# Two quarters of W_out laid out directly behind the second piece of y, in the first frame pair of the output projection

## The chip, the core and the metric

The kernel runs on one core of one Trainium2 chip. The time is the device time of one execution in microseconds (us), taken from the runs listed below; the profile is one further execution, recorded instruction by instruction. Engines are named as in the profile: PE is TensorE (PEld its weight loads), DVE is VectorE, ACT is ScalarE, POOL is GpSimd, SP is SyncE, which here only issues DMAs.

## The reference, cut to what matters

One layer of a streaming trunk is computed for 2048 prompt frames and 32 sample frames, all in float32:

```
proj = rmsnorm(h, g_mix) @ w_in              # 1024 -> 3072, split into hA bA cA zA vB zB
y    = concat[conv_mixer(hA, bA, cA, zA), pool_mixer(vB, zB)]      # 1024 wide
h    = h + y @ w_out                         # 1024 x 1024   <- the stage of this change
gate = sigmoid(rmsnorm(h, g_ple) @ w_ple_gate)
h    = h + (p @ w_ple) * gate
out  = rmsnorm(h, g_final)
```

The outputs are the normalised frames and the last rows of the two mixers' histories.

## The kernel before, in words

**Products.** Every float32 operand of a large product is split in two reduced-precision parts, hi and lo: ACT casts hi (`split`, L78), DVE subtracts it from the source for lo (L79). A product is then three matmuls: hi·hi, hi·lo, lo·hi. The 1024x1024 weight is cut into quarters 11, 12, 21 and 22, and two frame tiles of 128 frames are taken together, so that Strassen's scheme (Winograd's form) needs seven half products in place of eight. `frame_parts` (L181) makes the seven frame operands of a pair, called pieces here: the plain 11, 12, 22 and the sums S1 to S4. `weight_sums` makes the weight sums T1 to T4; the plain quarters 11, 21 and 22 of the weight are laid out without a sum.

**Order within a pair.** `seven` (L211) issues the products of one pair into three PSUM banks X, Y, Z, 12 matmuls each. With its argument late set and for the first pair (in_parts set) the order is:

1. X = piece 11 with W11 (L163); ACT copies X out (L1199), called here the first copy-out
2. the call of step 1, then half of Z = S1 with T1
3. X += S2 with T2; ACT copies X out again (L1199), the second copy-out
4. the rest of Z; third copy-out
5. X += S3 with T3, which may only begin when the second copy-out has read X; DVE adds X to the result (L1194)
6. Y = piece 12 with W21 (L163, named y_o in the profile): first the four hi·hi matmuls, then four lo·hi, then four that use the lo of W21; DVE adds Y to the result
7. Z += S4 with W22 (L163, z_o), in the same order of parts
8. X += piece 22 with T4 (L168, x_o<-wo_T), which may only begin when the add of item 5 has read X

Later pairs have the same products, all through L168.

**What the change touches.** `layout` casts and subtracts quarters of the weight: for each of four k, one ACT cast of 128x512 (L1266) and one DVE subtraction (L1267) for each quarter named. W11 is laid out first. The call of step 1 for the first pair is `rest`: it calls `more` (L204), which makes pieces 12, S4 and 22, and then lays out quarters 21 and 22, alternating between the two, eight casts and eight subtractions in all. In the profile the hi of W21 is in the tile wo_c, the lo of W21 and both parts of W22 in tiles named wo_d, the pieces are y (11, 12, 22) and y_S (S1 to S4).

**Who sets the order.** Each engine runs its own list of instructions in the order in which the program has them. That order comes from a planner, at build time: it goes through modelled time and gives an engine, when it comes free, the ready instruction that stands first in the kernel text. `tc.issue_after(ins)` pins every instruction that the block makes on the engine of `ins` behind `ins` on that engine; it holds nothing on other engines. In `rest` the ACT casts of the layout are pinned behind the cast of piece 22.

**Buffers.** The ring cmb has eight buffers of 4 KB a partition. Four hold the raw lower rows of W_out (wo_q, loaded at L323), the other four the pieces 11, S2, S1, S3, so piece 12 takes the buffer of 11 when the first product is through, S4 that of S2, and 22 that of S1. The pool w3, whose three tiles of 8 KB hold the lo of W21 and both parts of W22, is opened where the ring wr of the first stage lay (seven buffers of 4 KB); the tile for the lo of W22 lies on buffers of that ring from which the second and third output tile of the early embedding (eout) are still being stored to memory (L149). The upper and lower half of a pair's raw y are loaded by SP (L315) into a ring of five; the lower half of the first pair is read last when piece 22 is made, and its buffer then takes half of the third pair.

Of the kernel before, what the change touches and what calls it, by code (L numbers as in the profile page):

```python
# [12 lines left out]
ALU = mybir.AluOpType  # L13
# [22 lines left out]
def trunk(ctx, tc, x_p, x_s, c_conv, c_pool, p_p, p_s, g_mix, w_in, conv_w, conv_b, pool_w,  # L36
          pool_scale, w_out, g_ple, w_gate, w_ple, g_fin, y_p, y_s, sc_p, sp_p, sc_s, sp_s):
    nc = tc.nc
# [38 lines left out]
    def split(hi, lo, src, eng=nc.vector):  # L77
        ins = nc.scalar.copy(hi, src)  # L78
        eng.tensor_tensor(lo, src, hi.bitcast(F32), op=ALU.subtract)  # L79
        return ins  # L80
# [100 lines left out]
    def frame_parts(cmb, tmp, name, a11, a12, a21, a22):  # L181

        A = {}

        def put(q, src):
            A[q] = cmb.tile([P, KH, 2, P], F32R, tag="c", name=f"{name}_{q}")
            return split(A[q][:, :, 0], A[q][:, :, 1], src)  # L190

        def comb(q, x, y, op):
            t = tmp.tile([P, KH, P], F32, tag="s", name=f"{name}_f{q}")
            nc.vector.tensor_tensor(t, x, y, op=op)
            return t

        s1 = comb("S1", a21, a22, ALU.add)
        put("11", a11)
        s2 = comb("S2", s1, a11, ALU.subtract)
        put("S2", s2)  # L200
        put("S1", s1)
        put("S3", comb("S3", a11, a21, ALU.subtract))

        def more():  # L204
            put("12", a12)
            put("S4", comb("S4", a12, s2, ALU.subtract))
            return put("22", a22)

        return A, more

# [120 lines left out]
    with ExitStack() as s1:  # L331
# [17 lines left out]
        def put(piece, src):  # L349

            return split(piece[:, :, 0], piece[:, :, 1], src)
# [823 lines left out]
    with ExitStack() as s2:  # L1175
# [4 lines left out]
        def quarters(name, W):  # L1180
            c = halves(slot(f"{name}_c"))
            d = {h: w3.tile([P, KH, NH], F32R, tag=f"d{h}", name=f"{name}_d{h}") for h in (1, 0, 2)}
            W.update({"11": c[:2], "21": (c[2], d[0]), "22": (d[1], d[2])})
# [38 lines left out]
        def prep_h(i):  # L1222
            lo, hi = load_y(i, 2 * P) if i else first_y
            S[i], more = frame_parts(cmb, ss, f"y{i}", lo[:, :, :P], hi[:, :, :P], lo[:, :, P:], hi[:, :, P:])
            return more
# [35 lines left out]
        def layout(parts):  # L1261
            for k in range(KH):
                for q, t, c in ("11", tops[k // 2], k % 2), ("21", bots[k], 0), ("22", bots[k], 1):
                    if q in parts:
                        hi, src = W[q][0][:, k], t[:, c * NH:c * NH + NH]
                        nc.scalar.copy(hi, src)  # L1266
                        hold.append(nc.vector.tensor_tensor(W[q][1][:, k], src, hi.bitcast(F32), op=ALU.subtract))  # L1267

        quarters("wo", W)
        layout(["11"])  # L1270

        def rest():

            with tc.issue_after(more().ins):
                layout(["21", "22"])

        S = {}
        more = prep_h(0)
# [9 lines left out]
        for i in range(0, NT - 1, 2):  # L1288
# [5 lines left out]
            last = i + 4 == NT - 1  # L1294
# [3 lines left out]
            if i + 2 < NT - 1:  # L1298

                with tc.issue_after(loaded[-1].ins), tc.issue_after(hold[-1].ins):  # L1300
                    more = prep_h(i + 2)
# [367 lines left out]
```

## Time and profile before

| | us |
|---|---|
| three runs | 922.24, 920.8, 922.03 |
| median | 922.03 |
| the profiled execution, device time | 923.96 |
| its span, first to last instruction | 922.2 |
| PE busy in it | 907.6 |
| DVE, ACT, POOL busy in it | 723.1, 477.8, 149.9 |

The profiled execution is one run of its own: 1.76 us of its time lie outside the span. A row of the timeline gives the start, the length, the engine, the line of the kernel, the output and inputs and the number of instructions merged in it; in square brackets stands how long the engine had been idle before and what ended that. A row of the waits gives who waited for whom: the total in us, how often, the longest. Lengths of neighbouring instructions overlap by the pipeline's fill, so the distance between two starts is what an instruction costs in a row of its kind.

### The profile page before, as it was taken

The numbers are of one execution on the slowest core, as the hardware profiler recorded it, in microseconds if no ns is written. First come the engines' busy times: TensorE is split into PE (matmuls) and PEld (weight loads), VectorE is DVE, ScalarE is ACT, GpSimd is POOL, SyncE is SP. The second block draws the span as 40 slices with busy tenths as digits, with TensorE's granted clock in tenths as the row PEclk, the third lists the DMA queues.
The fourth block names the chain that finished last, engine by engine and source line by source line (L and its number), as shares of the span: only waits on it lengthen the run. The fifth ranks groups of instructions, "written<-read, shape, count | busy, mean of one in ns | idle before, by whom it ended". The sixth has DMA issues, their size and how long they took to land.

```text
span 922.2 us, 12940 instructions
## 1 busy us (share of the span) xinstructions
PE 907.6 (98%) x4485; PEld 820.7 (89%) x4485; DVE 723.1 (78%) x1231; ACT 477.8 (52%) x883; POOL 149.9 (16%) x271
## 2 busy tenths in 40 slices
PE   7999999999999999999999999999999999999996
PEld 5999999999999999999999987888877868888885
DVE  6896999999488989785777679665554799888975
ACT  6744565555335555443545456334334776465555
POOL 3111322212001111000000010111111002233333
PEclk9999999999999999999999999999999999999999
DMA  8345585769945546457655359755675876799883
GB/s 245 94 150 155 151 264 165 210 197 306 421 119 167 185 156 190 109 178 272 202 172 172 124 192 292 255 194 175 246 229 159 299 259 156 182 235 239 200 259 108
DMA packets 140734, 186.37 MB, mean 202 GB/s; under 512 B 12060, under 2 KB 111260, under 8 KB 139389
## 3 DMA queue, kind: packets, MB, share of 16 engines
q1 hardware_dynamic: 120237, 126.33, 44.7%
q0 software_dynamic: 17696, 53.71, 19.9%
q10 hardware_dynamic: 2736, 5.51, 1.8%
q8 instruction: 35, 0.57, 0.3%
q14 instruction: 30, 0.25, 0.1%
HBM read 128.93 MB, written 56.56 MB: 201 GB/s over the span
## 4 chain that ended last, share of the span: by engine, by line
PE 96%; ACT 1%; DVE 1%; DMA 1%; issue 0%; POOL 0%; SPq 0%; ACTq 0%; DVEq 0%; POOLq 0%
PE x_g L168 9%; PE x_o L168 9%; PE x_zbv L564 7%; PE x_ch L564 7%; PE x_zab L564 7%; PE e L103 5%; PE z_g L168 5%; PE z_o L168 4%; PE z_zbv L564 3%; PE z_ch L564 3%; PE z_zab L564 3%; PE v L564 3%; PE c L564 3%; PE b L564 3%; PE za L564 3%; PE h L564 3%
## 5 line engine op out<-in xcount | busy, mean ns | idle before, releaser
L78 ACT CAST y_S<-y_fS 128x512 fp32r<-128x512 f32 x32 | 19.5, 621 | 41.3 <-PE x_o L168 17.4
L103 PE MATMUL e<-wq,pps 128*128 128x512 f32 (+1 forms) x156 | 38.9, 399 | 0.2 <-ACT pps L78 0.2
L168 PE MATMUL x_o<-wo_b,y_S 128*128 128x512 f32 x128 | 35.7, 391 | 0.0
L168 PE MATMUL x_g<-wg_b,g_S 128*128 128x512 f32 x128 | 35.7, 389 | 0.0
L564 PE MATMUL z_zbv<-B,w_zbv_S 128*128 128x416 f32 x168 | 34.2, 352 | 0.0
L564 PE MATMUL x_ch<-B,w_ch_S 128*128 128x416 f32 x168 | 34.1, 351 | 0.0
L564 PE MATMUL z_zab<-B,w_zab_S 128*128 128x416 f32 x168 | 34.1, 351 | 0.0
L564 PE MATMUL x_zab<-B,w_zab_S 128*128 128x416 f32 x168 | 34.0, 351 | 0.0
L564 PE MATMUL x_zbv<-B,w_zbv_S 128*128 128x416 f32 x168 | 34.0, 351 | 0.0
L564 PE MATMUL z_ch<-B,w_ch_S 128*128 128x416 f32 x168 | 34.0, 350 | 0.0
L103 PEld LDWEIGHTS e<-wq,pps 128*128 128x128 f32 (+1 forms) x156 | 27.4, 182 | 6.9 <-ACT pps L78 0.5
L1396 POOL DMA_DIRECT2D e<-h_d x28 | 24.8, 907 | 51.1 <-DVE e L1393 42.3
L564 PEld LDWEIGHTS x_zab<-B,w_zab_S 128*128 128x128 f32 x168 | 31.3, 188 | 0.4
L564 PEld LDWEIGHTS x_zbv<-B,w_zbv_S 128*128 128x128 f32 x168 | 31.4, 188 | 0.3
L564 PEld LDWEIGHTS z_ch<-B,w_ch_S 128*128 128x128 f32 x168 | 31.4, 188 | 0.3
L564 PEld LDWEIGHTS z_zab<-B,w_zab_S 128*128 128x128 f32 x168 | 31.3, 188 | 0.3
L564 PEld LDWEIGHTS x_ch<-B,w_ch_S 128*128 128x128 f32 x168 | 31.3, 188 | 0.3
L564 PEld LDWEIGHTS z_zbv<-B,w_zbv_S 128*128 128x128 f32 x168 | 31.3, 188 | 0.4
L70 POOL TENSOR_SCALAR ms_x<-ssq_x 128x1 f32<-128x1 f32 (+2 forms) x18 | 10.7, 593 | 125.1 <-ACT junk L89 125.0
L78 ACT CAST y<-y 128x512 fp32r<-128x512 f32 x24 | 14.9, 619 | 29.3 <-PE z_o L168 12.8
L78 ACT CAST g_S<-g_fS 128x512 fp32r<-128x512 f32 x32 | 19.0, 618 | 18.6 <-DVE g_fS L1572 12.8
L168 PEld LDWEIGHTS x_o<-wo_b,y_S 128*128 128x128 f32 x128 | 24.0, 188 | 5.1 <-ACT c_o L1199 0.3
(592 smaller groups left out, 2656.6 us busy)
## 6 DMA issues: line engine op xcount, KB each, us to landing
y<-y_d SPq DMA_DIRECT2D x16, 512.0 KB, 5.6
x<-in_x_prompt_dram SPq DMA_DIRECT2D x16, 512.0 KB, 5.3
h_d<-x SPq DMA_DIRECT2D x16, 512.0 KB, 2.6
hn<-h_d SPq DMA_DIRECT2D x61, 128.0 KB, 6.5
xt<-in_x_prompt_dram SPq DMA_DIRECT2D x15, 512.0 KB, 6.1
e<-e_d SPq DMA_DIRECT2D x15, 512.0 KB, 6.0
e<-h_d POOLq DMA_DIRECT2D x28, 256.0 KB, 6.4
out_dram<-e POOLq DMA_DIRECT2D x13, 512.0 KB, 4.0
```

What stands on the lines that cost most here:

```text
L70: nc.gpsimd.tensor_scalar(ms[:n], ssq[:n], scalar1=1.0 / D, scalar2=EPS, op0=ALU.mult, op1=ALU.add)
L78: ins = nc.scalar.copy(hi, src)
L103: nc.tensor.matmul(ps[:n], pps[:, a, k, :n], wp[k][b][:, cs], start=k + q == 0, stop=k == 1 and q == 2)
L168: nc.tensor.matmul(ps[:n], lhs[:, k, a, :n], w[b][:, k], start=start and k + q == 0, stop=k == KH - 1 and q == 2, skip_group_check=True)
L564: nc.tensor.matmul(ps[:, :NB], lhs[:, k, x], b[:, k, y], start=start and k + q == 0, stop=stop and k == KH - 1 and q == 2, skip_group_chec ...
L1396: nc.gpsimd.dma_start(ee, h_d[r:r + P, at[1] * NH:at[1] * NH + NH], accum_op=ALU.add)
```

## The change

`more` takes a function that it calls between piece 12 and the pieces S4 and 22. For the first pair that is the layout of the quarters 21 and 22. Its ACT casts are pinned behind the cast of piece 12 and no longer behind that of piece 22; the ACT casts of S4 and 22 are pinned behind the last cast of the layout (`layout` now returns it). For the later pairs `more` is called without a function: there S4 and 22 are pinned behind 12.

```
-        def more():
-            put("12", a12)
-            put("S4", comb("S4", a12, s2, ALU.subtract))
-            return put("22", a22)
+        def more(then=None):
+            ins = put("12", a12)
+            if then:
+                with tc.issue_after(ins.ins):
+                    ins = then()
+            with tc.issue_after(ins.ins):
+                put("S4", comb("S4", a12, s2, ALU.subtract))
+                put("22", a22)
...
-                        nc.scalar.copy(hi, src)
+                        last = nc.scalar.copy(hi, src)
                         hold.append(nc.vector.tensor_tensor(W[q][1][:, k], src, hi.bitcast(F32), op=ALU.subtract))
+            return last
...
-            with tc.issue_after(more().ins):
-                layout(["21", "22"])
+            more(lambda: layout(["21", "22"]))
```

No instruction, byte or buffer is added or taken away.

## The prediction

> **What bounds the kernel now.** I read the page first.
>
> ```profile
> span 922.2 us, 12940 instructions
> ...
> PE 907.6 (98%) x4485; PEld 820.7 (89%) x4485; DVE 723.1 (78%) x1231; ACT 477.8 (52%) x883; POOL 149.9 (16%) x271
> ...
> PE 96%; ACT 1%; DVE 1%; DMA 1%; issue 0%; POOL 0%; SPq 0%; ACTq 0%; DVEq 0%; POOLq 0%
> ```
>
> PE is busy 98% of the span and is 96% of the chain that ended last. So a change of order, which adds no work, can only move PE's waits. The waits of PE in the whole span, and all waits between 546 and 570 us, where the first pair of W_out runs:
>
> ```profile
> PE pt L416 <- DVE xt L407: 2.9, 2, 2.3
> ...
> PE y_o L163 <- ACT wo_c L1266: 0.5, 1, 0.5
> ```
>
> ```profile
> PEld y_o L163 <- ACT wo_c L1266: 1.3, 2, 0.9
> ...
> PEld x_o L168 <- ACT c_o L1199: 0.3, 1, 0.3
> ```
>
> In this stage PE waits for two things: the layout's casts (item 6 of the order) and, a little, a copy-out. The row of 0.5 understates it, because the weight loads wait too. The true price comes from comparing stretches (columns: length, then busy time and count by engine, clock, DMA):
>
> ```profile
> 546.87:567.33 20.46, 19.91 (x86) 15.67 (x85) 17.50 (x29) 11.53 (x21) 1.98 (x3) 1.00 1.05 323
> 567.33:586.39 19.06, 19.06 (x86) 15.76 (x84) 16.49 (x27) 9.34 (x18) 3.13 (x6) 1.00 0.79 257
> ...
> 555.14:558.00 2.86, 2.86 (x13) 2.36 (x13) 2.78 (x6) 2.64 (x6) 0.00 (x0) 1.00 1.19 211
> 558.00:561.88 3.88, 3.33 (x14) 2.17 (x12) 3.88 (x7) 3.10 (x7) 0.00 (x0) 1.00 1.11 228
> 561.88:564.61 2.73, 2.73 (x14) 2.25 (x12) 2.72 (x6) 0.14 (x1) 0.00 (x0) 1.00 1.03 353
> ```
>
> The first pair takes 20.46 us, the second 19.06, at the same clock of 1.00: 1.40 us is all there is to win. A product of 12 matmuls takes 19.06 / 7 = 2.72. The stretch of y_o (558.00 to 561.88) takes 3.88: 1.16 too long. The one before it is 0.14 too long; 0.10 is spread over the rest.
>
> Why y_o is late is in the timeline, ACT first, then PE:
>
> ```profile
> 549.86 0.59 ACT L1199 COPY c_o<-x_o 128x512 f32<-128x512 f32 x1 [1.53 <-PE x_o L163]
> 550.35 0.62 ACT L78 CAST y<-y 128x512 fp32r<-128x512 f32 x1
> 553.99 0.62 ACT L78 CAST y_S<-y_fS 128x512 fp32r<-128x512 f32 x1 [3.02 <-PE x_o L168]
> 554.51 0.58 ACT L1199 COPY c_o<-x_o 128x512 f32<-128x512 f32 x1
> 555.36 0.62 ACT L78 CAST y<-y 128x512 fp32r<-128x512 f32 x1 [0.27 <-PE z_o L168]
> 555.88 0.62 ACT L1266 CAST wo_c<-wo_q 128x512 fp32r<-128x512 f32 x1
> 556.40 0.62 ACT L1266 CAST wo_d<-wo_q 128x512 fp32r<-128x512 f32 x1
> ...
> 559.53 0.62 ACT L1266 CAST wo_d<-wo_q 128x512 fp32r<-128x512 f32 x1
> ```
>
> ```profile
> 553.74 1.52 PE L168 MATMUL z_o<-wo_a,y_S 128*128 128x512 f32 x6
> 555.14 3.02 PE L168 MATMUL x_o<-wo_b,y_S 128*128 128x512 f32 x12
> 558.00 1.14 PE L163 MATMUL y_o<-wo_c,y 128*128 128x512 f32 x3
> 559.67 1.45 PE L163 MATMUL y_o<-wo_c,y 128*128 128x512 f32 x5 [0.54 <-ACT wo_c L1266]
> ...
> 564.61 2.88 PE L168 MATMUL x_o<-wo_T,y 128*128 128x512 f32 x12
> ```
>
> Piece 12 is cast at 550.35. Then ACT stands idle 3.02 us, because the next in its list, S4, wants the buffer of S2. S4 is cast at 553.99, the second copy-out runs at 554.51, piece 22 waits for S1's buffer until 555.36, and only behind it come the eight casts, 0.52 apart (555.88 to 556.40). The hi of W21 for the last k is the seventh, from 555.88 + 6 x 0.52 = 559.0 on; PE wants it at about 558.00 + 3 x 0.23 = 558.7.
>
> **The change part by part.** *The eight casts* (L1266, no DMA among them) move into the idle time. Their start is 550.35 + 0.52 = 550.87 and their end 550.87 + 8 x 0.52 = 555.03, so every hi of W21 and W22 is there before y_o at 558. Their raw rows must have landed:
>
> ```profile
> 541.00 1.97 SPq L323 DMA_DIRECT2D wo_q<-in_w_out_dram  x4
> ```
>
> ```profile
> DMA to landing us min/median/max: 3.6/4.6/5.5
> ```
>
> The last issue ends at 542.97; with the longest landing 548.5, over 2 us early. Term: -1.16, if all of y_o's excess goes; bounds 0 and -1.40.
>
> *What is late next on ACT.* The casts are longer than the hole: it ended at 553.99, they end at 555.03. The second copy-out stands last in the text, and S4 is ready with it, so I expect S4 at 555.03 and the copy-out at 555.55: 1.04 later than its 554.51. If piece 22 also gets ahead (its buffer frees at 555.26, when z_o ends), 1.56 later; if the copy-out comes straight behind the casts, 0.52; if it gets between them, nothing. The x_o at 555.14 has no slack: the 0.3 above is its wait for this copy-out. So as PE's list stands now the price is +0 to +1.56. But PE's list is planned too, and y_o, with all its hi casts done, is ready in that gap. That the planner fills so is in the trace of an earlier stage, where the transpose pst stands ahead of product b in the text, was late, and came after eight of its matmuls:
>
> ```profile
> 533.49 1.76 PE L564 MATMUL b<-hn,w_b 128*128 128x416 f32 x8
> 535.08 0.27 PE L988 MATMUL pst<-ident,st 128*34 128x128 f32 x1
> 535.11 3.27 PE L564 MATMUL b<-hn,w_b 128*128 128x416 f32 x16
> ```
>
> I take +0.16 for a cut product and imperfect filling, near the lower end because of these rows; both ends stay in the range.
>
> *S4 and 22 behind the casts.* Piece S4 is cast about 1 us later, 22 about 0.7 to 1.2. They are wanted by z_o (before: 561.88) and by x_o<-wo_T (564.61): over 4 us of cover, cost 0. The third copy-out comes earlier.
>
> *DVE.* The eight subtractions follow the casts. One of them meets a new wait: the lo of W22 goes where an embedding tile is still being stored.
>
> ```profile
> 548.32 0.55 POOL L149 DMA_DIRECT2D e_d<-eout  x1 [10.34 <-ACT y_S L78]
> ```
>
> ```profile
> e_d<-eout POOLq DMA_DIRECT2D x1, 512.0 KB, 7.1
> ```
>
> ```profile
> 557.22 0.69 DVE L1267 TENSOR_TENSOR wo_d<-wo_q,wo_d 128x512 fp32r<-128x512 f32 x1
> ...
> 560.84 0.68 DVE L1267 TENSOR_TENSOR wo_d<-wo_q,wo_d 128x512 fp32r<-128x512 f32 x1
> 561.44 0.68 DVE L1194 TENSOR_TENSOR x<-x,c_o 128x512 f32<-128x512 f32 x1
> ...
> 562.69 0.68 DVE L1194 TENSOR_TENSOR x<-x_o,x 128x512 f32<-128x512 f32 x1
> ```
>
> Before, that subtraction ran at 557.22, past the landing at 548.32 + 7.1 = 555.4. Now its cast is done by 552, and DVE stands at it until 555.4. Queued behind: seven subtractions counting itself, then S4's and 22's, two adds of copies, the add of Y, and the add of X. At 0.60 apiece (557.22 to 560.84 is six steps) the add of X starts at 555.4 + 12 x 0.60 = 562.6, as before (562.69). The lo of W21 is complete at 555.4 + 6 x 0.60 = 559.0, 559.1 with the pipeline; PE wants its last part at 558.00 + 11 x 0.23 = 560.5. The add of X must end, at 563.3, before x_o<-wo_T may start, which starts at 564.61 now: at best 1.3 earlier. So DVE costs nothing at a gain of 1.16, but it caps the gain.
>
> *SP.* No DMA moves in the text. But the load of the lower half for the third pair waits for piece 22's subtraction, which followed the cast of 555.36 and now comes at about 560.3; it waits at the head of SP's queue:
>
> ```profile
> 555.65 1.48 SPq L315 DMA_DIRECT2D y<-y_d  x2
> 565.90 0.33 SPq L1220 DMA_DIRECT2D h_d<-x  x1
> ```
>
> ```profile
> y<-y_d SPq DMA_DIRECT2D x2, 512.0 KB, 11.7
> ```
>
> ```profile
> 570.86 0.68 DVE L194 TENSOR_TENSOR y_fS<-y,y 128x512 f32<-128x512 f32 x1
> ```
>
> It goes out at about 561 instead of 556.8. Its first reader runs at 570.86. At the landing time of 11.7 it would come at 572.7, 1.8 too late; I take nothing, since 11.7 is the half queued behind two loads of x, and half the bytes of that backlog are gone by 561. SP's next issue is due at 565.90, past that. POOL gets and loses nothing. Later pairs already cast in the order 12, S4, 22, so their pins cost 0.
>
> **Sum.** -1.16 + 0.16 = -1.0. The profiled execution's 923.96 would be 922.96. Its time is 1.93 above the median of the runs, 922.03, so for the median I say 921.0.
>
> **The rivals.** *The copy-out binds* (0.22). PE keeps its list, x_o waits for the copy-out behind eight casts and one or two pieces: +1.04 to +1.56 against -1.16 to -1.30, hence -0.26 to +0.40, a median of 921.8 to 922.4. For it: the copy-out had no slack before. Against it: the filling rows. [...]
>
> *DVE held by the store* (0.10, the slower side). The place is the first subtraction of W22's lo; the price is one us for each us that the store lands after 555.4, as the whole list behind it, with the add of X at its end, shifts. From a landing at 556.7 on, nothing is left of the gain. At the 11.7 us that the y loads take it would land at 560.0: +4.6 - 1.2 = +3.4, or 925.4. For it: DMA share stands over 1.0 in these stretches. Against: the store is issued before anything that moves, so 7.1 should hold.
>
> *The late half for the third pair* (0.06): DVE is held at 570.86 for up to 1.8, of which PE feels at most 1.3: net about +0.3, 922.3.
>
> *The change does not do what it says* (0.05): the casts come no earlier, 922.0. Only missing raw rows could do it.
>
> **How the numbers follow.** Forecast 0.57: 921.0, by its own bounds (-1.40 to -0.5) 920.6 to 921.5. Runs of before lie 1.4 apart, so a median may be off by some 0.6. The range 919.9 to 923.0 leaves out the far part of the DVE rival and unlucky draws. A measurement of this kernel tells some 0.2%, 1.84 us, from no change; the whole excess of the pair is 1.40, so faster by more needs a further gain or luck: 0.11. Slower by more is the DVE rival past 558.5, or a knock-on of the new plan: 0.08. Within: 0.81.
>
> **What would show it.** Right: casts of L1266 from about 550.9 to 555.0 behind the cast of y; no wait of y_o on wo_c; the stretch of the first pair at 19.2 to 19.9 us. The copy-out rival shows as x_o (L168) waiting for ACT c_o by about 1 us with y_o behind it. The DVE rival shows as an idle time ahead of a wo_d subtraction ended by e_d's DMA and a late x_o<-wo_T. What would make me wrong: a PE wait outside this pair that before did not have, from a different plan downstream.

## The result, and the profile after

| | before | after |
|---|---|---|
| median of 8 runs each, us | 922.13 (920.8 to 923.77) | 926.09 (924.79 to 928.84) |
| ratio to before, 95% interval | | 1.0045 (1.003 to 1.006) |
| profiled execution, its span | 923.96, 922.2 | 925.96, 924.2 |

The change makes the kernel slower by about 4.0 us, outside the range of the prediction. The head of the page after shows no more work; PE is busy for 906.0 us where it was 907.6:

```profile
span 924.2 us, 12940 instructions
...
PE 906.0 (98%) x4485; PEld 818.9 (89%) x4485; DVE 722.8 (78%) x1231; ACT 477.1 (52%) x883; POOL 151.5 (16%) x271
```

The waits of PE between 540 and 595 us name what is new. The wait of y_o for the weight's casts is gone, and three others stand in its place:

```profile
PE x_o L168 <- DVE c_o L1198: 1.9, 1, 1.9
PE x_o L168 <- ACT c_o L1203: 1.0, 1, 1.0
PE x_o L168 <- DVE x L1198: 0.7, 1, 0.7
```

The same stretches as before, by the starts of the pairs, and then the second pair in pieces. The columns are the window, its length, busy time and count of PE, PEld, DVE, ACT and POOL, then the granted clock, the DMA share and GB/s:

```profile
544.72:566.10 21.38, 19.70 (x86) 15.67 (x85) 17.03 (x28) 11.63 (x22) 1.98 (x3) 1.00 1.01 305
566.10:588.98 22.88, 20.96 (x86) 16.83 (x84) 17.08 (x28) 10.74 (x20) 3.89 (x7) 0.93 0.68 223
...
570.20:572.26 2.06, 0.14 (x2) 0.00 (x1) 2.06 (x5) 2.06 (x5) 1.21 (x2) 1.00 0.93 267
572.26:574.00 1.74, 1.74 (x5) 1.39 (x6) 1.74 (x3) 0.88 (x2) 0.02 (x1) 0.69 0.96 272
574.00:575.30 1.30, 1.30 (x4) 0.99 (x3) 0.01 (x1) 0.00 (x0) 0.00 (x0) 0.50 1.04 340
```

The first pair takes 21.38 us (20.46 before), the second 22.88 (19.06): together +4.74. The larger part lies in the second pair. There the change only pins the casts of S4 and 22 behind that of 12, and ACT has these casts in the same order before and after. The spans differ by only 2.0, mainly because the first pair of the profiled execution of before began 2.15 later, at 546.87; the other 0.6 lies behind the two pairs. In the fourteen profiles of this study the first pair begins between 544.72 and 547.29. The sum of the two pairs is free of that, and is the measure used below; each is read from one profiled execution.

**First pair.** ACT, then DVE, then PE of the kernel after:

```profile
548.72 0.61 ACT L1270 CAST wo_c<-wo_q 128x512 fp32r<-128x512 f32 x1
...
552.36 0.62 ACT L1270 CAST wo_d<-wo_q 128x512 fp32r<-128x512 f32 x1
554.02 0.62 ACT L78 CAST y_S<-y_fS 128x512 fp32r<-128x512 f32 x1 [1.04 <-DVE wo_d L1271]
554.55 0.61 ACT L78 CAST y<-y 128x512 fp32r<-128x512 f32 x1
555.07 0.58 ACT L1203 COPY c_o<-x_o 128x512 f32<-128x512 f32 x1
```

```profile
553.29 0.69 DVE L1271 TENSOR_TENSOR wo_d<-wo_q,wo_d 128x512 fp32r<-128x512 f32 x1 [2.88 <-DMA e_d<-eout]
...
561.29 0.69 DVE L194 TENSOR_TENSOR y_fS<-y,y 128x512 f32<-128x512 f32 x1 [1.28 <-DMA y<-y_d]
561.90 0.69 DVE L79 TENSOR_TENSOR y<-y,y 128x512 fp32r<-128x512 f32 x1
562.51 0.68 DVE L1198 TENSOR_TENSOR x<-x_o,x 128x512 f32<-128x512 f32 x1
...
571.52 0.69 DVE L1198 TENSOR_TENSOR c_o<-x_o,x 128x512 f32<-128x512 f32 x1
```

```profile
552.95 1.75 PE L163 MATMUL y_o<-wo_c,y 128*128 128x512 f32 x7
555.70 3.01 PE L168 MATMUL x_o<-wo_b,y_S 128*128 128x512 f32 x12 [1.00 <-ACT c_o L1203]
...
563.25 3.02 PE L168 MATMUL x_o<-wo_T,y 128*128 128x512 f32 x12 [0.68 <-DVE x L1198]
...
572.26 0.50 PE L168 MATMUL x_o<-wo_a,y_S 128*128 128x512 f32 x1 [1.92 <-DVE c_o L1198]
```

The casts run in the old hole of ACT, from 4.00 us after the pair's start on. But the second copy-out comes behind S4 and 22, 10.35 us after the start (555.07 - 544.72; before 554.51 - 546.87 = 7.64). S4 stands ahead of it for 1.04 us, ended by a subtraction of the layout on DVE. From this release I infer that in the program after, S4 has the buffer of a raw row of the weight, wo_q, and no longer that of S2: that row is read last by the subtraction at 553.29, which stood 2.88 us for the embedding's store. The planner did fill PE: seven matmuls of y_o go ahead. They end at 552.95 + 7 x 0.227 = 554.54, so x_o (S3) is still 555.70 - 554.54 = 1.16 late. Then piece 22 with T4 is 563.25 - (559.69 + 2.72) = 0.84 late (z_o begins at 559.69): the add of X (562.51) now stands behind the first sum of the second pair's y, which waits for its load until 561.29. Before, that sum stood behind the add. Together 1.16 + 0.84 = 2.00 come in place of the 1.16 of y_o and 0.14 of the old copy-out. That is 0.70 of the 0.92 by which this pair is longer; the other 0.2 is spread.

**Second pair.** Two more adds now stand behind that sum, and four operations for the second and third pair stand ahead of the first carry c_o (571.52), which is the 17th operation behind it. In the kernel before (below) it was the 11th, and it waited for PE, not PE for it:

```profile
563.38 0.69 DVE L194 TENSOR_TENSOR y_fS<-y,y 128x512 f32<-128x512 f32 x1
...
570.25 0.69 DVE L1194 TENSOR_TENSOR c_o<-x_o,x 128x512 f32<-128x512 f32 x1 [0.17 <-PE x_o L168]
```

After the change PE has done all it can by 568.82 + 6 x 0.227 = 570.18 and halts until 572.26, 2.08 us. (The trace's idle time, 1.92, is shorter by the overlap of lengths.) Then the clock falls, to 0.50 in the last window above: the twelve matmuls of x_o take until 576.71, 4.45 us for 2.72. 2.08 + 1.73 = 3.81 of the 3.82 by which this pair is longer. Whether the pins or the new place of the layout led the planner to this list of DVE, no run separates.

### The profile page after: what moved, and what is told of

The parts are those of the page before. It is cut to its first block, busy times and chain, and to the rows that moved or that the text cites. A ratio compares the mean times of both kernels' runs of the same rounds, so it can differ in the third digit from the quotient of the medians.

```text
span 924.2 us, 12940 instructions
## 1 busy us (share of the span) xinstructions
PE 906.0 (98%) x4485; PEld 818.9 (89%) x4485; DVE 722.8 (78%) x1231; ACT 477.1 (52%) x883; POOL 151.5 (16%) x271
## 4 chain that ended last, share of the span: by engine, by line
PE 93%; DVE 2%; DMA 2%; ACT 1%; issue 1%; POOL 1%; SPq 0%; DVEq 0%; ACTq 0%; POOLq 0%
PE x_g L168 9%; PE x_o L168 8%; PE x_zbv L568 7%; PE x_ch L568 7%; PE x_zab L568 7%; PE e L103 5%; PE z_g L168 5%; PE z_o L168 4%; PE z_zbv L568 3%; PE z_ch L568 3%; PE z_zab L568 3%; PE c L568 3%; PE b L568 3%; PE za L568 3%; PE h L568 3%; PE zb L568 2%
## 5 line engine op out<-in xcount | busy, mean ns | idle before, releaser
L1198 DVE TENSOR_TENSOR c_o<-x_o,x 128x512 f32<-128x512 f32 x14 | 9.7, 691 | 26.8 <-PE x_o L168 26.8
```

The lines of the kernel that those rows point to most:

```text
L1198: add = lambda o, a, b: nc.vector.tensor_tensor(o, a, b, op=ALU.add)
```

## The experiments

Theories: **ORDER**, the new order of DVE's list around the landing of the second pair's y makes the second pair late (its most natural ground, that the planner's modelled load lands earlier than the real one, is an inference; no profile shows the planner's clock). **COPY-OUT**, the second copy-out behind S4 and 22 makes the first pair late. **HOLD**, all comes from S4's hold by the subtraction and the store. **CLOCK**, the second pair's last 1.7 us are the price of the halt itself. The first four runs stood beside one median of before, 923.11.

**e1: the order kept.** The change with DVE's order of the second pair pinned: pieces S4 and 22 of that pair and all of the third's behind the first carry.

```
+                ins = add(t[:n], ps[:n], half_of(x, at, n))
+                firsts.setdefault(name, ins)
...
+        def behind_first():
+            with tc.issue_after(firsts["o2"].ins):
+                later[-1]()       # S4 and 22 of the second pair, called at its step 1
...
+                behind = firsts[f"o{i}"] if i == 2 else hold[-1]
+                with tc.issue_after(loaded[-1].ins), tc.issue_after(behind.ins):
                     more = prep_h(i + 2)
```

> The changed kernel, with the vector engine's list in the second pair put right: the making of the third pair's sums, and of pieces S4 and 22 of the second pair, is pinned behind the first carry of the second pair. Theory ORDER (the loss sits in the second pair, because that carry stands behind four to six other vector operations, PE waits 1.9 us for it and then runs 4 us at half clock): second pair back from 22.9 to about 19.1 us, granted clock 1.00 throughout, first pair unchanged at 21.4, total 922.3. Theory HOLD (the vector engine simply runs late since it stood 2.9 us at the store of the embedding tile): the carry stays late whatever the order, second pair still over 21, total 924 to 926. Theory COPY-OUT (the second copy-out on ACT behind S4 and 22 starts it all): as HOLD, total 925 to 926.

```profile
547.29:568.93 21.64, 19.57 (x85) 15.68 (x85) 17.06 (x29) 11.68 (x22) 1.99 (x3) 1.00 0.98 303
568.93:588.15 19.22, 19.22 (x86) 15.69 (x84) 16.87 (x28) 8.82 (x16) 3.46 (x6) 1.00 0.78 258
```

Measured 923.97, ratio 1.0018 (1.0005 to 1.003). The second pair is back at 19.22, the clock at 1.00. The first stays at 21.64, with one wait of PE, for the copy-out:

```profile
559.35 3.01 PE L168 MATMUL x_o<-wo_b,y_S 128*128 128x512 f32 x12 [2.07 <-ACT c_o L1211]
```

So ORDER explains the second pair, and something else the first. The two pairs together are 1.34 over before, the median 0.86, where I had expected 0.2 (922.3 beside 922.13).

**e2: quarter by quarter.** The change with all casts and subtractions of W21 ahead of those of W22, so that the subtraction that waits for the store comes later in the list.

```
-            for k in range(KH):
-                for q, t, c in ("11", tops[k // 2], k % 2), ("21", bots[k], 0), ("22", bots[k], 1):
+            for p in parts:
+                for k in range(KH):
```

> The changed kernel, with the layout quarter by quarter: the four casts and subtractions of 21, then the four of 22. The subtraction that waits for the embedding tile's store is then the fifth, and the hold shrinks from 2.9 to about 0.5 to 1 us. Theory HOLD: both pairs recover, first pair about 20, second about 19.1, total 921 to 922. Theory ORDER: the first pair gains about 1 us (S4 no longer waits for a buffer that this subtraction frees), the second stays at 22 to 22.9, total about 925. Theory COPY-OUT: first pair gains at most what S4's wait of 1.0 cost, second unchanged, total 925.

```profile
547.28:568.64 21.36, 19.72 (x86) 15.67 (x86) 17.04 (x29) 11.77 (x22) 1.99 (x3) 1.00 0.98 305
568.64:589.92 21.28, 19.38 (x86) 15.69 (x85) 17.07 (x28) 10.73 (x20) 3.89 (x7) 1.00 0.72 240
```

Measured 926.15, ratio 1.0049 (1.0031 to 1.0067): no gain. DVE no longer stands for the store at all. The wait for the copy-out falls from 1.00 to 0.53, but that of T4 rises from 0.68 to 1.12: DVE, free earlier, now stands 3.01 for the second pair's y, with the add of X behind it. The first pair stays at 21.36. HOLD falls as the root. One thing is told by the way: the second pair halts for 1.91 us as in the kernel after, yet its clock stays at 1.00, and it is 1.6 shorter (21.28 against 22.88).

**e3: the copy-out first.** The change with S4 and 22 of the first pair made at step 3, so behind the second copy-out in the text.

```
+            def others():
+                with tc.issue_after(ins.ins):
+                    put("S4", comb("S4", a12, s2, ALU.subtract))
+                    put("22", a22)
+            if then:
+                return others
...
-            more(lambda: layout(["21", "22"]))
+            later.append(more(lambda: layout(["21", "22"])))
...
-{0: {1: rest}, 2: {3: next_gate}}
+{0: {1: rest, 3: lambda: later[0]()}, 2: {3: next_gate}}
```

> The changed kernel, with pieces S4 and 22 called behind the second copy-out, so that ACT's list is piece 12, eight casts, copy-out, S4, 22. Theory COPY-OUT: x_o with S3 starts about 2 us earlier in the first pair, and all that is late behind it comes back: first pair about 19.6, second 19.1, total 921. Theory ORDER: first pair about 19.6 to 20, but the carry of the second pair still stands behind four operations: second pair 21.5 to 22.9, total 923 to 924.5. Theory HOLD: the vector engine's hold of 2.9 us stays, total 924 to 926.

```profile
545.31:564.75 19.44, 19.44 (x85) 15.76 (x85) 16.29 (x27) 10.91 (x21) 1.99 (x3) 1.00 1.04 323
564.75:588.36 23.61, 20.96 (x85) 16.83 (x84) 17.82 (x29) 11.47 (x21) 3.89 (x7) 0.93 0.67 226
```

Measured 926.54, ratio 1.0052 (1.0033 to 1.007). The first pair is at 19.44, 1.02 under before: the gain that the prediction worked out is real. The second pair is worse than ever, 23.61, and worse than ORDER had it (21.5 to 22.9), with a halt of 2.65 and the clock at 0.93.

**e4: both.** The edits of e1 and e3 together.

> The changed kernel with both edits: copy-out ahead of S4 and 22, and the second pair's vector list put right. The hold at the store stays in. Theory ORDER with COPY-OUT as the cause of the first pair's part: first pair 19.5 to 20, second 19.1, total 920.8 to 921.5, that is 0.6 to 1.3 faster than the kernel before. Theory HOLD: no better than 923.5.

```profile
545.33:564.73 19.40, 19.40 (x86) 15.76 (x85) 15.77 (x26) 10.48 (x20) 1.98 (x3) 1.00 1.05 322
564.73:584.69 19.96, 19.33 (x86) 15.69 (x84) 18.08 (x30) 9.96 (x18) 3.62 (x6) 1.00 0.80 259
```

Measured 922.43, ratio 0.9995 (0.9982 to 1.0007). The two causes make the whole loss: without them the kernel is where it was, within what can be measured. But the gain that I expected is not there: 1.06 won in the first pair leaves only 39.52 - 39.36 = 0.16 in both, as the second pair takes 19.96 and not 19.1. DVE of e4:

```profile
561.78 0.69 DVE L194 TENSOR_TENSOR y_fS<-y,y 128x512 f32<-128x512 f32 x1 [0.44 <-DMA y<-y_d]
...
568.40 0.68 DVE L1206 TENSOR_TENSOR c_o<-x_o,x 128x512 f32<-128x512 f32 x1
```

The load lands 16.45 us after the start of the first pair (561.78 - 545.33), and from there DVE works without a gap to the carry at 568.40. PE gets to the point where it needs the carry 1.06 sooner than before, the carry does not: PE waits 0.63.

**e5 and e6: the third sum late.** e4 with the lo of S3 of the second pair behind the first carry too (e5), and that with the layout quarter by quarter (e6, the edit of e2).

```
+        s3 = comb("S3", a11, a21, ALU.subtract)
+        if not third_late:
+            put("S3", s3)
...
+                if third_late:
+                    put("S3", s3)      # ahead of S4 in others
```

> This is the kernel with the copy-out ahead and VectorE's order kept, with one step more: the subtraction that makes the sum S3 of the second pair's y goes behind the first carry of that pair too, so that the carry stands one operation earlier behind the landing of y. ORDER: the 0.63 us that the second pair's products still waited for that carry go, and no other wait takes their place: first pair 19.4 us, second pair 19.2 to 19.4 (19.06 before), both 38.6 to 38.8 against 39.52 before; time 0.6 to 1.0 us under before, ratio 0.999. LANDING (what counts is when the y load of the second pair lands, 14 us after its issue, and everything on VectorE runs on from there without a gap): the wait moves to another product of the pair, second pair 19.8 to 20.0 as in the run before, time within 0.3 us of before.

> The same, and the two quarters of the weight are cast and subtracted one after the other, as before the change, and not all casts first. If the hold of ScalarE by S4 were of weight (HOLD), this would be under the run with the casts first by the 0.5 to 1.5 us that ScalarE gets back; with the copy-out in front of S4 and of quarter 22 (COPY-OUT) nothing waits behind them any more, and the two runs agree within 0.5 us: first pair 19.2 to 19.6, second 19.2 to 19.6.

```profile
545.85:565.21 19.36, 19.36 (x86) 15.76 (x86) 15.28 (x26) 9.99 (x20) 1.98 (x3) 1.00 1.05 324
565.21:585.09 19.88, 19.37 (x85) 15.69 (x84) 18.43 (x31) 10.39 (x19) 4.22 (x6) 1.00 0.80 258
```

```profile
564.17:584.54 20.37, 19.34 (x86) 15.69 (x85) 18.93 (x31) 10.92 (x19) 4.22 (x6) 1.00 0.77 247
```

Measured 922.05, ratio 0.9994 (0.9983 to 1.0004), and 922.44, ratio 1.0001 (0.9991 to 1.0012), beside 922.2. The wait of 0.5 stays although an operation of 0.6 left the list: the load of y landed at 562.73, 16.9 after the start. That is what LANDING expected. The first pair of e6 is 19.35, so HOLD is worth nothing once the copy-out is in front; its second pair, 20.37, lies outside what I expected of it, and there y landed only 17.4 after the start (562.23 - 544.82). (The expectation of e6 calls its order that of before; it is that of e2, four casts of W21 and then four of W22, where before alternated.)

**e7 and e8: a halt by itself.** The kernel before, nothing of the change: the first carry's add of the second pair is written once more (e7) or three times more (e8), and product Z of that pair is held in its place in PE's list so that PE has to stand.

```
                 add(t[:n], ps[:n], half_of(x, at, n))
+                if name == "o2" and at == (0, 0):
+                    for _ in range(1):          # e8: 3
+                        add(t[:n], ps[:n], half_of(x, at, n))
```

> The kernel before with nothing of the change, but the first carry's addition of the second pair is done twice (the same sum is written again, so the output stays) and TensorE's product Z of that pair is held in its place in the list, so that TensorE has to stand still for the carry, which it did not before. CLOCK (a halt of some 2 us by itself lets the granted clock fall to about a half for some 4 us, as in the second pair behind the change): a halt of 1 to 3 us shows, and in the 5 us behind it the granted clock is 0.5 to 0.7 and the pair is longer than by the halt alone, by 1 to 2 us. OTHER CAUSE (the half clock came from something else around the change, such as the run of weight loads): the halt shows, the clock stays at 1.00 behind it, and the pair is longer by the halt alone.

> The same with the addition done four times: a halt of 4 us and more. CLOCK: the granted clock falls to 0.5 for 3 us or more behind the halt, the pair is longer by the halt and 1.5 to 2 us. OTHER CAUSE: clock 1.00, longer by the halt alone.

Windows of e7, then of e8: the second pair, the halt, what follows it. The halt of e8 is ended by a cast on ACT and not by the carry.

```profile
565.99:590.30 24.31, 20.88 (x85) 16.83 (x84) 18.08 (x29) 11.24 (x21) 3.27 (x7) 0.93 0.65 216
568.80:572.29 3.49, 0.07 (x1) 0.03 (x1) 3.49 (x7) 2.90 (x5) 0.94 (x2) 1.00 0.97 329
572.29:574.00 1.71, 1.71 (x5) 1.32 (x6) 1.66 (x3) 0.56 (x1) 0.00 (x0) 0.55 1.05 334
574.00:575.50 1.50, 1.50 (x5) 1.21 (x4) 0.69 (x1) 0.06 (x1) 0.00 (x0) 0.50 1.00 326
```

```profile
565.19:591.66 26.47, 20.79 (x86) 16.75 (x84) 18.85 (x30) 10.74 (x21) 3.31 (x7) 0.87 0.58 191
568.00:573.75 5.75, 0.07 (x1) 0.03 (x1) 5.64 (x10) 3.48 (x6) 0.55 (x1) 0.68 0.91 285
573.75:575.50 1.75, 1.75 (x4) 1.46 (x5) 1.05 (x2) 0.00 (x0) 0.00 (x0) 0.50 0.99 366
```

One execution each, 928.16 and 929.54. Against 19.06 the pairs are longer by 5.25 and 7.41. Counted like the 2.08 above, the halts are 572.29 - (565.99 + 2.72) = 3.58 and 573.75 - (565.19 + 2.72) = 5.84, both longer than that one. So 1.67 and 1.57 us come on top, at a clock of 0.50, with none of the change in the kernel. CLOCK holds so far: a halt by itself can take the clock down, at about the price of 1.73 that the kernel after paid. But not every halt of 2 us does it: that of e2 (1.91 us, clock 1.00) did not, nor did two more in the last section.

**e9 and e10: the gate rows later.** e5, and the kernel before, with the loads of each gate row (two of 256 KB, the first at 550.3 us in e5) meant to go behind the second pair's first carry, and a step later each.

```
+            with tc.issue_after(firsts["o2"].ins):
                 for half, t in enumerate(ts):
                     nc.gpsimd.dma_start(t, rows[:, :, half * NH:half * NH + NH])
...
-            next_gate()
+            if i:
+                next_gate()            # and one call more at step 3 of the third pair
```

> The kernel with the copy-out ahead, VectorE's order kept and the third sum late, and the two 256 KB loads of the first gate row (issued at 550.3 us, in the stretch where the DMA engines are busy at a share of 1.0 and more) go behind the first carry of the second pair; every later gate row comes half a pair or a pair later than now, and one call more makes up for it in the third pair. LANDING (the y load of the second pair, which landed 13.3 us after its issue, sets the second pair, so that the microsecond won in the first pair cannot go through): 512 KB less in this stretch, at the 215 to 420 GB/s that its windows show, let y land 1.2 to 2.4 us sooner, the wait of 0.51 us for the first carry goes, the second pair takes 19.0 to 19.3 us (19.88 in the run before this one) and the time is 0.6 to 1 us shorter than that kernel's, ratio to the kernel before 0.998 to 0.9985. VECTORE (its number of operations ahead of the carry sets the second pair, whatever lands): second pair 19.7 to 20.0, time as before, ratio 0.9994.

> The kernel before, with nothing of the change but the same delay of the gate rows. LANDING: in the kernel before, TensorE waited for nothing in the second pair (19.06 us), so that an earlier y wins nothing there: within 0.3 us of the kernel before, ratio 0.9995 to 1.0005; this tells whether a gain of the run beside it comes from the gate rows by themselves.

Measured 925.57, ratio 1.0032 (1.002 to 1.0045), and 925.36, ratio 1.0035 (1.002 to 1.005), beside 922.73. Neither is what I expected, because the edit does not do what it was meant to do. The carry is an instruction of DVE, the loads are issued by POOL, and `tc.issue_after` holds nothing on another engine. The first gate row goes out long before y lands, in e9 (second line) as in e5 (first line). Only the later rows move, the second row from 580.05 in e5 to 591.00 (third line):

```profile
550.26 1.43 POOL L1262 DMA_DIRECT2D gs<-in_w_ple_gate_dram  x2 [2.41 <-DMA e_d<-eout]
```

```profile
548.55 1.45 POOL L1263 DMA_DIRECT2D gs<-in_w_ple_gate_dram  x2 [1.39 <-PE x_o L163]
591.00 1.45 POOL L1263 DMA_DIRECT2D gs<-in_w_ple_gate_dram  x2 [3.62 <-issue]
```

Both are slower alike: in the third pair ACT stands for that row (below, e10), DVE behind it, and PE then waits for DVE, 1.58 and 0.63 us in e10, 2.03 and 0.82 in e9.

```profile
599.58 0.72 ACT L1253 ACTIVATE gs<-gs,vec 128x512 f32<-128x512 f32 x1 [6.34 <-DMA gs<-in_w_ple_gate_dram]
```

Whether y lands sooner without the 512 KB has no answer here. In e9 it landed 561.95 - 545.17 = 16.8 us after the start of the pair, but the 512 KB were still in the stretch.

```profile
561.95 0.69 DVE L194 TENSOR_TENSOR y_fS<-y,y 128x512 f32<-128x512 f32 x1 [0.88 <-DMA y<-y_d]
```

My estimate of 1.2 to 2.4 us is untested, and what sets the landing of this load, 13.3 us after its issue in e5 and 14.1 in the kernel after by the chain of waits, stays open; the gate row is one candidate.

**e11 and e12: piece 12 late too.** e5 with piece 12 of the second pair behind the first carry (e11); and this order of DVE in the kernel before, with the layout where it was (e12).

```
-                    later.append(others)
+                    later.append(lambda more=more: more())    # 12, S3, S4, 22
```

> The kernel with the copy-out ahead, VectorE's order kept and the third sum late (gate rows as in the kernel before), and the piece 12 of the second pair's y is made behind the first carry too, so that one subtraction more (0.60 us) stands behind the carry. VECTORE (from the landing of y on VectorE works without a gap, and the number of its operations ahead of the carry sets the second pair): the wait of 0.51 us for the carry goes, second pair 19.2 to 19.4 us (19.88 with the third sum alone), first pair 19.4, time 0.5 us under that kernel's, ratio to the kernel before 0.9985 to 0.999. LANDING (the load of y alone): the wait stays at 0.4 to 0.6 us, second pair 19.8, ratio 0.9994.

> The kernel before with the layout where it was, and only the order of the run beside it on VectorE (second pair: first carry ahead of piece 12, of the sums S3 and S4, of quarter 22 and of the third pair's sums). If the gain of the run beside it is the change's (the wait of 0.54 us for the weight's cast and what goes with it), this kernel keeps that wait, first pair 20.4 us and second 19.1, and its time is that of the kernel before within 0.3 us, ratio 0.9995 to 1.0003; if it is the order's, both gain alike.

```profile
544.89:564.28 19.39, 19.39 (x85) 15.75 (x85) 14.66 (x25) 9.46 (x18) 1.98 (x3) 1.00 1.06 319
564.28:584.16 19.88, 19.37 (x85) 15.63 (x84) 19.09 (x32) 10.91 (x19) 6.05 (x6) 1.00 0.76 252
```

```profile
562.44 0.69 DVE L194 TENSOR_TENSOR y_fS<-y,y 128x512 f32<-128x512 f32 x1 [1.54 <-DMA y<-y_d]
```

```profile
545.28:565.72 20.44, 19.87 (x85) 15.68 (x85) 17.50 (x29) 11.46 (x21) 1.99 (x3) 1.00 1.04 322
565.72:584.96 19.24, 19.24 (x85) 15.63 (x84) 16.45 (x27) 8.71 (x17) 2.92 (x6) 1.00 0.79 249
```

Measured 922.56, ratio 0.9992 (0.9982 to 1.0002), and 923.46, ratio 1.0006 (0.9997 to 1.0015), beside 922.69. e11 (first two fences): one operation fewer again, the same pair of 19.88, because y landed only 562.44 - 544.89 = 17.55 us after the start. The wait stays, as LANDING had it and VECTORE had not. But the carry runs where the landing and the list behind it put it, 11 operations in e4, 10 in e5 and 9 in e11, and each time the landing came later by about what one operation takes (16.45, 16.90, 17.55): the carry starts 23.07, 22.91 and 22.96 us after the start of the first pair. Whether that is chance, one profile of each cannot tell. e12 (last fence) keeps y_o's wait and 20.44: the order alone wins nothing. No version here is faster than before by more than can be measured; the best, e5 and e11, have intervals that end at 1.0004 and 1.0002.

## Why the prediction was wrong, point by point

- **The eight casts, -1.16: right.** They start 4.00 us after the pair (predicted 550.87 - 546.87 = 4.00), y_o waits for nothing. e3 to e6 and e11 have the first pair at 19.35 to 19.44, 1.0 to 1.1 under before.
- **The copy-out, +0.16: mis-sized.** The step that failed is "I expect S4 at 555.03": it took S4's buffer as free, and that of S2. In the program after, S4 was released only by a subtraction of DVE behind the store; it stood 1.04, and 22 went ahead as well. The copy-out came 2.71 us later than before, where I had 1.56 at most. The order on PE was mended in the gap, as the rows of product b suggested, but seven matmuls (1.59 us) did not cover 2.71. The term measured 1.16 for 0.16, and e3, which puts the copy-out first, takes it away. The rival "the copy-out binds" had the size right (1.04 to 1.56), but not the way: it had PE keep its list, and PE's list was filled.
- **"DVE costs nothing": failed.** The store landed 7.13 us after its issue (predicted 7.1), so the rival of the held DVE did not happen. What I had added up was the list of before: a sum for the second pair now stands in front of the add of X, and it waits for a load, at a price of 0.84 us. In e3 the add stands ahead of that sum again, and the wait is gone. In e1 the sum still stands in front; no wait shows there, as PE had already stood 2.07 us for the copy-out.
- **"Later pairs ... cost 0": failed, and this is most of the loss.** With DVE's order kept the pins cost little (19.22 in e1 against 19.06), but the program was planned anew behind them, and DVE's list of the second pair changed: 2.08 us of halt and 1.73 of slow clock. e1 takes both away with nothing but the order. The prediction named this as what would make it wrong, "a PE wait outside this pair", and gave it no price of its own, only a share of the 0.08 for slower by more.
- **What the gain could be at most: not seen.** I took 1.40 as "all there is to win" from the first pair alone. With both causes away 0.16 to 0.28 us are left (e4, e5), because the second pair's y lands 16.45 to 17.55 us after the first pair's start in e4, e5, e6, e9 and e11, where the first pair is short, and no later, 16.5 to 16.8, in the kernel after, e1 and e2, where it is 2 us longer. The carry follows the landing. A bound has to be taken from the next late arrival, too.
- The term for the third pair's half load (0) was right: DVE makes the third pair's first sum at 569.11 without a wait for the load.

## What to carry to other kernels

Where a planner sets the order from modelled time, a pin is a new plan for everything behind it: compare the lists of all engines in the next stage, and look for an instruction that waits for a DMA and has moved ahead of work that PE wants. A microsecond won in one stage is worth only what the next arrival (here a load) lets through. A halt of PE of some 2 us cost almost twice its length where it took the clock down (in the kernel after 2.08 us, and 1.73 on top of it at a clock of 0.50), as one of four such halts here did. And before a run is read as an answer, look in its trace whether the edit moved what it was meant to move: in e9 it did not.

## What the runs showed of the hardware

The granted clock fell to 0.50 at some short halts of PE and stayed up at others of the same length. By the trace's idle times, halts of 1.92 (after), 2.65 (e3), 3.43 (e7) and 5.68 us (e8) took it down. Halts of 0.51 (e5), 0.63 (e4), 1.03 (e6), 1.91 (e2), 2.07 (e1, first pair, shown above) and 2.03 us (e9, third pair, here) left it at 1.00:

```profile
602.95 3.01 PE L168 MATMUL x_o<-wo_T,y 128*128 128x512 f32 x12 [2.03 <-DVE x L1210]
```

So near 2 us the length alone does not decide, and what does, these runs do not show.

The price did not grow with the halt. Read by windows of 0.1 us, the clock was at 0.50 from 572.9 to 576.3 in the kernel after, for 3.4 us, and as long in e3 and e7. In e8 it was down for 6.8 us, from 570.05 on, 3.7 of them within the halt. The twelve matmuls behind the halt take 2.72 us at full clock; they took 4.45 (after), 4.44 (e3), 4.42 (e7) and 4.28 (e8). That is 1.73, 1.72, 1.70 and 1.56 on top, about half of the time that they spent at 0.50.
